# Log-sum-exp over rows: the first load read as one block, its results stored early, and the semaphores cleared under the last store

## The chip, the cores and the metric

The kernel runs on one core of a Trainium2 chip. The metric is the device time of one execution in microseconds (us); less is better. The span that the profile shows runs from the first to the last instruction of the program; the time is about 1.8 us longer.

Engines are named as in the profile: ACT is ScalarE, DVE is VectorE, POOL is GpSimd, SP is SyncE; a name with a q (SPq) is that engine's queue of DMA issues, waits and semaphore instructions.

## The reference

```python
x = np.random.randn(32, 512, 1024).astype(np.float32)      # 67.1 MB
def reference(x, axis):                                    # axis = -1
    x_max = np.max(x, axis=axis, keepdims=True)
    return (x_max.squeeze(axis) + np.log(np.sum(np.exp(x - x_max), axis=axis))).astype(np.float32)
```

There are 16,384 rows of 4 KiB, and one number comes out of each. The kernel leaves the maximum out and computes log(sum(exp(x))) directly.

## The kernel before

Partition p owns rows 128p to 128p+127 (`p t` below), so the same row number of two neighbouring partitions lies 512 KiB apart in HBM. The rows come in 17 chunks of 16 down to 1 rows per partition, all loaded by SP into a ring of 51 rows. For each chunk ACT takes the exponential; the first `n_dve` rows are summed by DVE, the others by ACT itself (`accum_out`). Two logarithms turn the sums into results: the first covers chunks 0 to 4 and is taken when chunk 5 starts, the second covers the rest. One store writes everything.

```python
CHUNKS = [(4, 1), (15, 11), (16, 10), (16, 15), (16, 0), (14, 0), (12, 9), (9, 5), (7, 5), (5, 4),
          (4, 3), (3, 0), (2, 2), (2, 2), (1, 0), (1, 0), (1, 0)]       # (rows, of them for DVE)
x_v = x_flat.rearrange("(p t) d -> p t d", p=P)
out_v = bass.AP(tensor=out.tensor, offset=out.offset, ap=[[NB, P], [1, NB]])      # NB = 128
landed = [tc.alloc_semaphore(f"landed{i}") for i in range(len(CHUNKS))]           # and three more
# ... (cut: load(i) waits on SP until the ring's rows are free, then issues chunk i)
nc.sync.dma_start(out=ring[:, s : s + r], in_=x_v[:, row : row + r]).then_inc(landed[i], 16)
# ... (cut: exponentials, sums, logarithms)
nc.scalar.dma_start(out=out_v, in_=res).then_inc(stored, 16)
nc.gpsimd.wait_ge(stored, 16)
# the tile context closes: barrier, clear its semaphores, barrier
```

The softmax here doesn't subtract the row's maximum and nothing guards it: scores larger than these inputs give would overflow.

Of the kernel before, what the change touches and what calls it, by code (L numbers as in the profile page):

```python
# [1 line left out]

# [4 lines left out]



CHUNKS = [  # L10
    (4, 1), (15, 11), (16, 10), (16, 15), (16, 0), (14, 0), (12, 9), (9, 5), (7, 5), (5, 4),
    (4, 3), (3, 0), (2, 2), (2, 2), (1, 0), (1, 0), (1, 0),
]
RING_ROWS = 51

LN_AT = 5

FIRST_PARTS = [("sync", 0, 128)]


@with_exitstack
def kernel(
    ctx: ExitStack,
    tc: tile.TileContext,
    x: bass.AP,
    axis: bass.AP,
    out: bass.AP,
):
    nc = tc.nc
    P = nc.NUM_PARTITIONS  # L30

    assert axis in (-1, len(x.shape) - 1), f"only last-axis reduction supported, got {axis}"

    x_flat = x.flatten_outer_dims()
    N, D = x_flat.shape
    assert N % P == 0
    NB = N // P
    assert sum(r for r, _ in CHUNKS) == NB

    fp32 = mybir.dt.float32  # L40
    Exp = mybir.ActivationFunctionType.Exp
    Ln = mybir.ActivationFunctionType.Ln
    AX = mybir.AxisListType.X

    x_v = x_flat.rearrange("(p t) d -> p t d", p=P)
    out_v = bass.AP(tensor=out.tensor, offset=out.offset, ap=[[NB, P], [1, NB]])

    ring = nc.alloc_sbuf_tensor("ring", [P, RING_ROWS, D], fp32).ap()
    sums = nc.alloc_sbuf_tensor("sums", [P, NB], fp32).ap()
    res = nc.alloc_sbuf_tensor("res", [P, NB], fp32).ap()  # L50

    landed = [tc.alloc_semaphore(f"landed{i}") for i in range(len(CHUNKS))]
    act_done = tc.alloc_semaphore("act_done")
    dve_done = tc.alloc_semaphore("dve_done")
    stored = tc.alloc_semaphore("stored")


    hook = nc.pop_inst_callback()
    symbolic, nc._always_lower_symbolic_ap = nc._always_lower_symbolic_ap, False


    place = []
    row = slot = 0
    for r, _ in CHUNKS:
        if slot + r > RING_ROWS:
            slot = 0
        place.append((slot, row))
        slot += r
        row += r



    busy = [(0, 0)] * RING_ROWS
    acts = dves = 0

    def load(i):
        (s, row), r = place[i], CHUNKS[i][0]
        act_wait = max(a for a, _ in busy[s : s + r])
        dve_wait = max(d for _, d in busy[s : s + r])
        if dve_wait:  # L80
            nc.sync.wait_ge(dve_done, dve_wait)
        if act_wait:
            nc.sync.wait_ge(act_done, act_wait)
        for engine, lo, hi in FIRST_PARTS if i == 0 else [("sync", 0, P)]:
            getattr(nc, engine).dma_start(
                out=ring[lo:hi, s : s + r], in_=x_v[lo:hi, row : row + r]
            ).then_inc(landed[i], 16)

    def take_logs(lo, hi, dve_wait, act_wait):
        nonlocal acts  # L90
        nc.scalar.wait_ge(act_done, act_wait)
        nc.scalar.wait_ge(dve_done, dve_wait)
        nc.scalar.activation(out=res[:, lo:hi], in_=sums[:, lo:hi], func=Ln).then_inc(  # L93
            act_done, 1
        )
        acts += 1

    body = nc.main_func.blocks[-1]
    assert not body.instructions
    load(0)  # L100
    n_early = len(body.instructions)

    nc.scalar.preload_act_table_set("natural_log_exp_and_others")  # L103

    logged = 0
    done_before = [(0, 0)]
    for i, (r, n_dve) in enumerate(CHUNKS):
        if i:
            load(i)
        s, row = place[i]  # L110
        if i == LN_AT:
            logged = row
            take_logs(0, logged, *done_before[i])
        nc.scalar.wait_ge(landed[i], 16 * (len(FIRST_PARTS) if i == 0 else 1))
        if n_dve:
            nc.scalar.activation(  # L116
                out=ring[:, s : s + n_dve], in_=ring[:, s : s + n_dve], func=Exp
            ).then_inc(act_done, 1)
            acts += 1
            nc.vector.wait_ge(act_done, acts)  # L120
            nc.vector.reduce_sum(  # L121
                out=sums[:, row : row + n_dve], in_=ring[:, s : s + n_dve], axis=AX
            ).then_inc(dve_done, 1)
            dves += 1
            for j in range(n_dve):
                busy[s + j] = (0, dves)
        for j in range(n_dve, r):
            nc.scalar.activation(  # L128
                out=ring[:, s + j],
                in_=ring[:, s + j],  # L130
                func=Exp,
                accum_out=sums[:, row + j : row + j + 1],
            ).then_inc(act_done, 1)
            acts += 1
            busy[s + j] = (acts, 0)
        done_before.append((dves, acts))

    take_logs(logged, NB, dves, acts)
    nc.scalar.wait_ge(act_done, acts)
    nc.scalar.dma_start(out=out_v, in_=res).then_inc(stored, 16)  # L140
    nc.gpsimd.wait_ge(stored, 16)



    first = nc.main_func.blocks[0]
    head, work = first.instructions, body.instructions
    end = next(k for k, i in enumerate(head) if i.opcode == "UnconditionalBranch")
    head, tail = head[:end], head[end:]
    for ins in work[:n_early]:
        at = next(  # L150
            k for k, i in enumerate(head) if i.engine == ins.engine and i.opcode == "Drain"
        )
        head.insert(at, ins)
    first.instructions = head + work[n_early:] + tail
    body.instructions = []

    nc._always_lower_symbolic_ap = symbolic
    nc.push_inst_callback(hook)


# [1 line left out]
_INS = ['x', 'axis']  # L162
_OUTS = [((32, 512), 'float32')]

_NUMBERS = {'axis': -1}


# [26 lines left out]
```

## Time and profile before

| | before |
|---|---|
| time, median of the first 3 runs | 164.23 us (164.02 to 164.56) |
| span of the profiled run | 162.18 us |
| chunk 0 landed | 7.40 us |
| chunk 4 landed; ACT without idle time from here on | 83.67 us |
| chunk 16, the last, landed | 158.08 us |
| last store issued; GpSimd past its wait | 159.64; 161.24 us |
| end of the closing barriers | 162.18 us |

The landing times are those of the last of each load's 16 semaphore steps in the trace. First come lines of the profile's page, for the whole run: the busy engines, then the DMA queues with packets, MB and their share of 16 engines' span.

```profile
span 162.2 us, 213 instructions
...
DVE 72.9 (45%) x11; ACT 124.1 (76%) x136; POOL 0.2 (0%) x4
...
q1 hardware_dynamic: 2448, 67.11, 96.4%
q10 hardware_dynamic: 144, 0.07, 0.1%
q14 instruction: 1, 0.01, 0.0%
```

The load queue q1 is busy for 96.4% of the span, and ACT for 76%. The next view is the chain of waits in order of time (start us, us, what).

```profile
47.15 36.52 DMA ring<-in_x_dram
83.67 0.02 issue
83.69 10.55 ACT ring L128 x21
...
156.21 2.71 ACT ring L128 x5
158.91 0.22 issue
159.14 0.20 ACT ring L128
```

The chain goes through loads until chunk 4 lands, then through ACT. That looks like an ACT-bound second half. But the loads run level with it: the last chunk lands at 158.08 us and ACT takes it at 158.19. Now the stage table around the events that the change touches (stretch, its length, busy time with counts of DVE, ACT and POOL, clock, DMA share, GB/s). The table counts a packet's bytes where the packet starts, so a short stretch is to be compared with the same stretch of another run and not with a rate.

```profile
0.70:2.70 2.00, 0.00 (x0) 1.28 (x1) 0.00 (x0) 1.00 0.77 262
...
147.00:149.00 2.00, 2.00 (x1) 2.00 (x2) 0.00 (x0) 1.00 0.95 399
```

Last, the close, as instructions of the line that ends the kernel (duration in ns min/median/max, first and last start in us).

```profile
L189 POOLq EVENT_SEMAPHORE  x4: 17/17/17, 161.5 to 162.1; - x4
...
L189 POOLq COMPARE_BRANCH  x1: 33/33/33, 161.2 to 161.2; - x1
L189 POOLq EVENT_SEMAPHORE_RANGE_CLEAR  x1: 139/139/139, 161.7 to 161.7; - x1
```

Four semaphore instructions of GpSimd are two barriers, a gather and a release each, with the range clear between them. From GpSimd's passing at 161.24 us to the end it takes 0.94 us.

### The profile page before, as it was taken

What the parts mean: (1) busy time and instruction counts of PE and PEld (TensorE: products, weight loads), DVE (VectorE), ACT (ScalarE), POOL (GpSimd) and SP (SyncE); (2) the same over time, 40 slices, a digit from 0 to 9 for tenths busy, and PEclk for the clock granted to TensorE, in tenths of its full rate; (3) what the DMA queues carried; (4) which work ended last, traced back from release to release, by engine and by line L of the source; (5) the groups of instructions that cost most, each with busy time, mean ns of one, the idle gap of its engine ahead of it and who ended that gap; (6) DMA issues with size and microseconds to landing.
All of it is one profiled execution on the core that took longest, in us unless ns stands there. A gap on an engine that the chain in (4) does not pass through costs nothing.

```text
span 162.2 us, 213 instructions
## 1 busy us (share of the span) xinstructions
DVE 72.9 (45%) x11; ACT 124.1 (76%) x136; POOL 0.2 (0%) x4
## 2 busy tenths in 40 slices
DVE  0030000039960799000999900000006999799591
ACT  3180006997099971999339999999999999999993
POOL 0000000000000000000000000000000000000000
DMA  6999899969969959969988999999999999999970
GB/s 263 497 485 470 349 394 517 485 291 517 485 291 517 517 259 517 517 275 501 517 368 370 424 424 432 461 497 388 436 427 399 431 400 439 420 424 414 415 318 16
DMA packets 2593, 67.18 MB, mean 414 GB/s; under 512 B 288, under 2 KB 416, under 8 KB 800
## 3 DMA queue, kind: packets, MB, share of 16 engines
q1 hardware_dynamic: 2448, 67.11, 96.4%
q10 hardware_dynamic: 144, 0.07, 0.1%
q14 instruction: 1, 0.01, 0.0%
HBM read 67.11 MB, written 0.07 MB: 414 GB/s over the span
## 4 chain that ended last, share of the span: by engine, by line
ACT 52%; DMA 38%; DVE 7%; issue 1%
DMA ring<-in_x_dram 38%; ACT ring L128 30%; ACT ring L116 22%; DVE sums L121 7%; ACT res L93 0%
## 5 line engine op out<-in xcount | busy, mean ns | idle before, releaser
L121 DVE TENSOR_REDUCE sums<-ring 128x5 f32<-128x5120 f32 (+8 forms) x11 | 72.9, 6648 | 86.0 <-ACT ring L116 85.9
L116 ACT ACTIVATE ring<-ring 128x5120 f32<-128x5120 f32 (+8 forms) x11 | 59.3, 5394 | 29.4 <-DMA ring<-in_x_dram 29.4
L128 ACT ACTIVATE ring<-ring 128x1024 f32<-128x1024 f32 x61 | 63.4, 1041 | 5.3 <-DMA ring<-in_x_dram 5.3
L128 ACT ACTIVATION_READ_ACCUMULATOR ring<-ring 128x1 f32 x61 | 11.4, 187 | 0.0
L103 ACT ACT_TABLE_LOAD x1 | 1.3, 1283 | 0.8 <-PEq L175 0.8
L93 ACT ACTIVATE res<-sums 128x67 f32<-128x67 f32 (+1 forms) x2 | 0.5, 256 | 0.1
L175 POOL MEMSET const-bfloat16-1.0<- 128x1 bf16 x1 | 0.1, 101 | 0.0
L175 POOL MEMSET const-uint8-127<- 128x1 uint8 x1 | 0.1, 101 | 0.0
L175 POOL MEMSET const-float32-0.0<- 128x1 f32 x1 | 0.1, 98 | 0.2 <-issue 0.2
L175 POOL MEMSET const-float32-1.0<- 128x1 f32 x1 | 0.1, 98 | 0.0
## 6 DMA issues: line engine op xcount, KB each, us to landing
ring<-in_x_dram SPq DMA_DIRECT2D x1, 7680.0 KB, 24.8
ring<-in_x_dram SPq DMA_DIRECT2D x1, 7168.0 KB, 36.1
ring<-in_x_dram SPq DMA_DIRECT2D x1, 6144.0 KB, 21.6
ring<-in_x_dram SPq DMA_DIRECT2D x1, 4608.0 KB, 32.1
ring<-in_x_dram SPq DMA_DIRECT2D x2, 2048.0 KB, 26.3
ring<-in_x_dram SPq DMA_DIRECT2D x1, 3584.0 KB, 40.2
ring<-in_x_dram SPq DMA_DIRECT2D x1, 2560.0 KB, 44.4
ring<-in_x_dram SPq DMA_DIRECT2D x2, 1024.0 KB, 46.0
```

What stands on the lines that cost most here:

```text
L93: nc.scalar.activation(out=res[:, lo:hi], in_=sums[:, lo:hi], func=Ln).then_inc(act_done, 1)
L103: nc.scalar.preload_act_table_set("natural_log_exp_and_others")
L116: nc.scalar.activation(out=ring[:, s : s + n_dve], in_=ring[:, s : s + n_dve], func=Exp).then_inc(act_done, 1)
L121: nc.vector.reduce_sum(out=sums[:, row : row + n_dve], in_=ring[:, s : s + n_dve], axis=AX).then_inc(dve_done, 1)
L128: nc.scalar.activation(out=ring[:, s + j], in_=ring[:, s + j], func=Exp, accum_out=sums[:, row + j : row + j + 1],).then_inc(act_done, 1)
L175: nc = _bacc.Bacc("TRN2", target_bir_lowering=False, num_devices=1)
```

## The change

The intent: make the first load contiguous so that it starts faster; get the results of its rows out early; and clear the semaphores while the last store is on its way, so that less is left to do after it. Chunk 0 is now rows 0 to 511 of the input (rows 4p to 4p+3 for partition p, one block of 2 MB); the other rows follow at 508 KiB pitch. So the results fall into two pieces of the output, stored as 16-byte and as 496-byte rows, packed one after another.

```diff
-    x_v = x_flat.rearrange("(p t) d -> p t d", p=P)
-    out_v = bass.AP(tensor=out.tensor, offset=out.offset, ap=[[NB, P], [1, NB]])
+    R0 = CHUNKS[0][0]                                                    # 4
+    x_first = x_flat[: P * R0].rearrange("(p t) d -> p t d", p=P)
+    x_rest = x_flat[P * R0 :].rearrange("(p t) d -> p t d", p=P)
+    out_first = bass.AP(tensor=out.tensor, offset=out.offset, ap=[[R0, P], [1, R0]])
+    out_rest = bass.AP(
+        tensor=out.tensor, offset=out.offset + P * R0, ap=[[NB - R0, P], [1, NB - R0]]
+    )
...
-    landed = [tc.alloc_semaphore(f"landed{i}") for i in range(len(CHUNKS))]
+    landed = [nc.alloc_semaphore(f"landed{i}") for i in range(len(CHUNKS))]   # the others likewise
...
+        if i == STORE_AT:                                                # 11, ahead of load(11)
+            nc.sync.wait_ge(act_done, logs_done)
+            nc.sync.dma_start(out=out_first, in_=res[:, :R0]).then_inc(stored_first, 16)
         if i:
             load(i)
...
-    nc.scalar.dma_start(out=out_v, in_=res).then_inc(stored, 16)
-    nc.gpsimd.wait_ge(stored, 16)
+    nc.scalar.dma_start(out=out_rest, in_=res[:, R0:]).then_inc(stored, 16)
+    nc.scalar.sem_clear(range(used[0], used[-1] + 1))
+    for sem in (stored_first, stored):
+        nc.gpsimd.wait_ge(sem, 16)
+        nc.gpsimd.sem_inc(sem, -16)
```

More of the change, by code (lines that the diff above doesn't have):

```diff
@@ L16 @@
 LN_AT = 5
-FIRST_PARTS = [("sync", 0, 128)]
+STORE_AT = 11
 @with_exitstack
@@ L43, with rows_of @@
     AX = mybir.AxisListType.X
-    x_v = x_flat.rearrange("(p t) d -> p t d", p=P)
-    out_v = bass.AP(tensor=out.tensor, offset=out.offset, ap=[[NB, P], [1, NB]])
+    R0 = CHUNKS[0][0]
[5 more added lines that the diff above has]
+    )
+    def rows_of(row, r):
+        return x_first if row == 0 else x_rest[:, row - R0 : row - R0 + r]
     ring = nc.alloc_sbuf_tensor("ring", [P, RING_ROWS, D], fp32).ap()
@@ L50 @@
     res = nc.alloc_sbuf_tensor("res", [P, NB], fp32).ap()
-    landed = [tc.alloc_semaphore(f"landed{i}") for i in range(len(CHUNKS))]
-    act_done = tc.alloc_semaphore("act_done")
-    dve_done = tc.alloc_semaphore("dve_done")
-    stored = tc.alloc_semaphore("stored")
+    landed = [nc.alloc_semaphore(f"landed{i}") for i in range(len(CHUNKS))]
+    act_done = nc.alloc_semaphore("act_done")
+    dve_done = nc.alloc_semaphore("dve_done")
+    stored_first = nc.alloc_semaphore("stored_first")
+    stored = nc.alloc_semaphore("stored")
+    used = sorted(sem.num for sem in [*landed, act_done, dve_done])
+    assert used == list(range(used[0], used[0] + len(used)))
     hook = nc.pop_inst_callback()
@@ L83, in load @@
             nc.sync.wait_ge(act_done, act_wait)
-        for engine, lo, hi in FIRST_PARTS if i == 0 else [("sync", 0, P)]:
-            getattr(nc, engine).dma_start(
-                out=ring[lo:hi, s : s + r], in_=x_v[lo:hi, row : row + r]
-            ).then_inc(landed[i], 16)
+        nc.sync.dma_start(out=ring[:, s : s + r], in_=rows_of(row, r)).then_inc(landed[i], 16)
     def take_logs(lo, hi, dve_wait, act_wait):
@@ L113 @@
             take_logs(0, logged, *done_before[i])
-        nc.scalar.wait_ge(landed[i], 16 * (len(FIRST_PARTS) if i == 0 else 1))
+            logs_done = acts
+        nc.scalar.wait_ge(landed[i], 16)
         if n_dve:
```

## The prediction

> **What bounds it now.** The span is 162.18 us; the run takes about 2 us more, outside it. From start to end the kernel is paced by one stream of loads: 67.11 MB of 67.18 moved, and the stage table gives 416, 436, 439, 426, 425 GB/s in the stages up to 116 us. From the trace's landings, the three 16-row chunks land 19.36, 19.39 and 19.33 us apart (8.39 MB each, 433 GB/s); a 61,440-byte packet takes 2.267 us, the same rate times 16. The chain of waits hands over to ScalarE at 83.69 us, when chunk 4 lands, and ScalarE is then busy until 159.61 (idle: 0.0x us). The two are level: in the timeline chunk 10 lands 0.13 us before ScalarE takes it, chunk 11 0.14, chunk 13 about 0.03, chunk 16 0.11. So a delay of the whole load stream passes to the end nearly one for one, and so does an advance. Before 7.42 us ScalarE waits for chunk 0, after 159.64 nothing but the store and the closing ceremony is left.
>
> **Terms.**
> 1. Chunk 0 as one block. Packets of 16,384 bytes take 0.611 us in the steady state, but the first two on each engine took up to 1.36 us; the excess sums to 5.9 us, 0.37 us per engine. Now rows lie 512 KiB apart. The Trainium skill, "DMA: Bandwidth & Descriptors", section "Latency and other measured facts", says that power-of-two row pitches slow copies (slightly at 512 KiB, much at megabytes), with aliasing of channels as an inference. This trace agrees only in the start: the steady rate is at full speed, so the 508 KiB pitch of the rest should gain nothing. I take 0.25 us of the 0.37 off; chunk 0 then lands at about 7.1 instead of 7.40, and chunk 4 and everything after moves with it. Critical.
> 2. The early store: 128 descriptors of 16 bytes in the load queue before chunk 11, 8 per engine. A 4-byte packet takes 9 ns, a 512-byte one 27 ns: estimate 0.07 to 0.25 us per engine, say 0.15, in a stream without slack. Critical, a cost.
> 3. The last store has rows of 496 bytes instead of 512. The same page, "Specifications", has a read-modify-write under 512 bytes; no run here shows it yet. Before: issue 159.64, landed 161.22. Estimate +0.1 us. Critical.
> 4. The close. After the landing GpSimd passes at 161.24, a first barrier ends at about 161.66, then a drain, a range clear (139 ns), a drain and a second barrier end at 162.18. With no semaphores of the context left to clear I expect clear and second barrier to go: -0.5 us (if the second barrier stays, only -0.17). GpSimd gains two decrements after its waits: +0.06. The clear on ScalarE (139 ns) after the issue at 160.01 hides under the 1.2 us until landing.
>
> Sum: -0.25 + 0.15 + 0.1 - 0.5 + 0.06 = -0.44 us.
>
> **Prediction:** 163.8 us, range 163.2 to 164.4. Faster by over 2%: 0.02; within 2%: 0.97; slower by over 2%: 0.01.
>
> **What would show it.** (1) First packets near 0.61 us, chunk 0 landing at 7.0 to 7.2, chunk 4 earlier by the same. (2) Chunk 10 to 11 landing gap 3.69 now, 3.8 to 3.9 after; small ScalarE idle times near chunks 11 to 16. (3) issue-to-landing of the last store 1.57 us now, 1.6 to 1.8 after. (4) one barrier after the landing, 0.45 us instead of 0.94 from GpSimd's passing to the end.
>
> **What would make it wrong.** The slow start is the cost of a cold engine and not of the pitch; tiny HBM writes stall the load ring by much more than their packets; partial rows in the last store take far longer; the second barrier stays; or the runs' own scatter (164.02 to 164.56) swallows 0.4 us.

## The result

The changed kernel took 164.51 us (median of 6 runs, 164.39 to 164.76), the kernel before in the same rounds and the earlier runs 164.43 us (6 runs, 164.02 to 164.56). The ratio is 1.0011 with a 95% interval of 0.9997 to 1.0024: no change at 2%, and if anything 0.1% slower. A ratio is always the mean time of one kernel's fast runs over that of the other's of the same rounds, so it is not quite the ratio of the medians. The predicted 163.8 us, with a range to 164.4, was too fast: the 0.44 us gain did not come.

The page after, the same lines:

```profile
span 162.8 us, 214 instructions
...
DVE 72.9 (45%) x11; ACT 124.2 (76%) x136; POOL 0.2 (0%) x4
...
q1 hardware_dynamic: 2592, 67.11, 96.6%
q10 hardware_dynamic: 144, 0.06, 0.1%
```

The engines do the same work. q1 has 144 more packets: the early store, 128 of data and 16 of semaphore. The chain of waits after:

```profile
64.87 36.40 DMA ring<-in_x_dram
101.28 0.02 issue
101.30 3.23 ACT ring L142 x6
104.53 0.02 issue
104.55 45.56 DMA ring<-in_x_dram
150.11 0.02 issue
150.13 3.23 ACT ring L142 x6
```

The chain now waits for loads at two places more, chunk 5 at 101.28 us and chunk 11 at 150.11 us. So the loads fell behind ACT. The stage table after:

```profile
0.70:2.70 2.00, 0.00 (x0) 1.28 (x1) 0.00 (x0) 1.00 0.93 197
...
147.00:149.00 2.00, 2.00 (x1) 2.00 (x2) 0.00 (x0) 1.00 1.01 346
```

Less moved in the first 2 us (197 against 262 GB/s), although the DMA engines are busy for more of it: the packets are stretched. Less is moved between 147 and 149 us too, in chunk 11, which follows the early store in the queue (346 against 399). The close:

```profile
L157 ACTq EVENT_SEMAPHORE_RANGE_CLEAR  x1: 119/119/119, 160.8 to 160.8; - x1
L160 POOLq EVENT_SEMAPHORE  x2: 17/17/17, 146.9 to 162.2; - x2
L208 POOLq EVENT_SEMAPHORE  x4: 17/17/17, 162.3 to 162.7; - x4
```

The clear has moved to ACT, at 160.8 us under the store. But GpSimd still has four semaphore instructions at the end: both barriers are still there. From GpSimd's passing at 162.17 us to the end it takes 0.68 us instead of 0.94.

Where the 0.66 us between these two profiles went, from landings and starts in the trace:

| event | before | after | later by |
|---|---|---|---|
| chunk 0 landed | 7.40 | 7.73 | 0.33 |
| chunk 4 landed | 83.67 | 83.94 | 0.26 |
| chunk 5 landed | 100.65 | 101.28 | 0.63 |
| chunk 10 landed | 145.61 | 146.23 | 0.62 |
| chunk 11 landed | 149.30 | 150.11 | 0.82 |
| chunk 16 landed | 158.08 | 158.85 | 0.77 |
| last store, issue to GpSimd's passing | 1.60 | 1.74 | 0.15 |
| from there to the end | 0.94 | 0.68 | -0.26 |

So there are three losses on the loads (start, between chunk 4 and 5, between chunk 10 and 11), one at the last store, and one gain. The pair of profiles overstates the difference: the runs' means differ by 0.18 us, while the profiled run before took 163.96 us, its fastest. The experiments therefore take more profiles of each layout and time each part.

One more reading is needed, by packet. The trace lists every DMA packet with start and duration. On each of the 16 engines one load packet follows another without a gap, so each engine's sequence can be followed through the run. The one exception is the instruction fetch: while its packet runs, 0.30 us long, its engine carries no load packet. In both kernels the load packet just after it, of chunk 5, is stretched as well:

```
kernel   instruction packet     load packet of chunk 5 (57,344 bytes, usual 2116 to 2120 ns)
before   89.05 us, 8,192 bytes  89.35 us, 2379 ns; its engine was the 3rd of 16 to finish chunk 4, 0.62 us ahead of the last
after    89.54 us, 8,192 bytes  89.85 us, 2498 ns; its engine was the 10th, 0.22 us ahead of the last
```

So the fetch costs its engine about 0.57 us before and 0.68 us after: 0.30 for itself, the rest for the stretched packet. The chunk lands later only by what exceeds that engine's lead over the last one: nothing before (0.57 against 0.62), 0.46 us after (0.68 against 0.22).

### The profile page after: what moved, and what is told of

It is laid out like the page before. It is cut to its first block, busy times and chain, and to the rows that moved or that the text cites. A ratio compares the mean times of both kernels' runs of the same rounds, so it can differ in the third digit from the quotient of the medians.

```text
span 162.8 us, 214 instructions
## 1 busy us (share of the span) xinstructions
DVE 72.9 (45%) x11; ACT 124.2 (76%) x136; POOL 0.2 (0%) x4
## 4 chain that ended last, share of the span: by engine, by line
DMA 77%; ACT 14%; DVE 7%; issue 0%; SPq 0%
DMA ring<-in_x_dram 77%; ACT ring L130 8%; DVE sums L135 7%; ACT ring L142 6%; SPq L97 0%; ACT res L103 0%
```

## The experiments

Two theories stood at the start. **A**: the losses belong to the change, each to one of its parts (block, tiny packed rows in the load queue, packed rows in the last store), and the fetch hurts because the block leaves its engine among the late ones. **B**: the losses are scatter of single runs, and the parts cost nothing. Each kernel got one profile; those with rounds were timed against the kernel before on the same chip. "Excess" is the duration of chunk 0's packets over 611 ns each, summed and divided by 16 engines.

| run | excess of chunk 0 | chunk 0 / chunk 4 landed | gap of landings, chunk 10 to 11, first step / last step | last store | close | ratio to before (95%) |
|---|---|---|---|---|---|---|
| before | 0.36 | 7.40 / 83.67 | 3.69 / 3.69 | 1.60 | 0.94 | |
| before_again | 0.47 | 7.42 / 83.75 | 3.69 / 3.71 | 1.60 | 0.94 | one look |
| close_only | 0.55 | 7.41 / 83.74 | 3.70 / 3.70 | 1.61 | 0.68 | 0.9982 (0.9969 to 0.9994) |
| old_rows | 0.58 | 7.30 / 83.88 | 3.71 / 3.71 | 1.60 | 0.68 | 0.9990 (0.9978 to 1.0002) |
| packed_stores | 0.56 | 7.57 / 83.88 | 3.75 / 3.95 | 1.64 | 0.68 | 1.0015 (0.9994 to 1.0036) |
| block_read_only | 0.83 | 7.61 / 83.79 | 3.69 / 3.69 | 1.60 | 0.94 | 1.0006 (0.9992 to 1.0020) |
| block_close | 0.82 | 7.69 / 83.86 | 3.69 / 3.68 | 1.61 | 0.68 | 0.9986 (0.9973 to 0.9999) |
| store_last | 0.91 | 7.58 / 83.77 | 3.68 / 3.69 | 1.74 | 0.68 | 0.9993 (0.9980 to 1.0006) |
| after | 0.94 | 7.73 / 83.94 | 3.89 / 3.88 | 1.74 | 0.68 | 1.0011 (0.9997 to 1.0024) |
| after_again | 0.84 | 7.68 / 83.87 | 3.93 / 3.71 | 1.74 | 0.68 | one look |

(Excess, landings, gaps, store and close in us, each from one profile.) The kernels that give wrong results are marked below. The comparison with the reference passed them all the same, because the rows' results lie too close together to tell rows apart; nothing here rests on their results.

### A second look at both kernels

No edit.

> A second profile of the kernel before, to see what is the kernel's and what is the run's. Theory A (the slow start and the lag belong to the layout): chunk 0 lands at 7.3 to 7.5 us, excess of the 16,384-byte packets of chunk 0 over 611 ns about 0.36 us per engine as in the first profile, and the instruction fetch of 8,192 bytes near 89 us costs nothing at chunk 5's landing (spread of its 16 semaphore steps about 0.7 us). Theory B (both are scatter of the run): chunk 0 lands anywhere from 7.2 to 7.9 us, and the spread of chunk 5 can be 1 us here too.

> A second profile of the changed kernel. Theory A: chunk 0 lands again at 7.6 to 7.8 us, excess 0.8 to 1.0 us per engine, chunk 5's landing again spread over about 1 us. Theory B: somewhere between 7.2 and 7.9 us with no relation to the kernel. Either way the landing gap of chunks 10 to 11 stays near 3.88 us (3.69 before) and the close takes 0.67 us from GpSimd's passing to the end.

Measured: theory A for the start. Chunk 0 landed at 7.42 us in the kernel before and at 7.68 us in the changed one; the excess was 0.47 and 0.84 us. For the lag at chunk 5 too: the fetch's engine was again the 3rd to finish chunk 4 before, 0.77 us ahead of the last, and the 10th after, 0.32 us ahead; it made chunk 5 late by 0.36 us after (its end against that of the latest other engine) and by nothing before. The last-to-last gap of chunks 10 to 11 was 3.71 us after, not 3.88 as expected, while the first-to-first gap was 3.93: the stall hits most engines, and how much of it reaches the last one varies. In this look the last engine was the one delayed by the fetch.

### The block alone

The kernel before with chunk 0 read from the first 2 MB (wrong: `x_0` holds rows of other partitions):

```diff
+    x_0 = x_flat[: P * 4].rearrange("(p t) d -> p t d", p=P)
-                out=ring[lo:hi, s : s + r], in_=x_v[lo:hi, row : row + r]
+                out=ring[lo:hi, s : s + r],
+                in_=x_0[lo:hi, 0:r] if i == 0 else x_v[lo:hi, row : row + r],
```

> The kernel before with one edit: chunk 0 is read from the first 2 MB as one block (wrong result on purpose, the rows are those of other partitions); stores, close and the other loads as before. Theory A: chunk 0 lands 0.25 to 0.35 us later than in the kernel before, and the time rises by 0.3 to 0.6 us (0.6 if the lag on one engine at chunk 5 comes with it). Theory B: same time within 0.15 us. The prediction's own theory (the block starts faster): time falls by 0.25 us.

Measured: 164.41 us (5 runs) against 164.28 (9 runs), ratio 1.0006 (0.9992 to 1.0020). The start is slow again (excess 0.83 us, chunk 0 at 7.61), and the fetch again meets an engine with a small lead (0.34 us) and costs 0.33 us in the profile. The 0.25 us gain that the prediction took for the block would be a ratio of 0.9985, which is outside the interval. But theory A's 0.3 to 0.6 us did not come either; the cost in time is small and not clear of zero.

### The close alone

```diff
-    stored = tc.alloc_semaphore("stored")       # the others likewise
+    stored = nc.alloc_semaphore("stored")
+    nc.scalar.sem_clear(range(used[0], used[-1] + 1))      # used: numbers of all of them but `stored`
     nc.gpsimd.wait_ge(stored, 16)
+    nc.gpsimd.sem_inc(stored, -16)
```

> The kernel before with only the new way of clearing semaphores. From the profile after: GpSimd's passing to the end 0.67 instead of 0.94 us, so the time falls by 0.25 us (0.15%); the store's issue to landing stays at 1.57 us. If the gain of the close is eaten by the decrement behind the wait or by the clear on ScalarE: no change.

Measured: 164.00 us against 164.28, ratio 0.9982 (0.9969 to 0.9994), clear of no change. The close took 0.68 instead of 0.94 us and the store 1.61 us. The lines of its close:

```profile
L193 POOLq EVENT_SEMAPHORE  x4: 17/17/17, 161.6 to 162.0; - x4
...
L143 ACTq EVENT_SEMAPHORE_RANGE_CLEAR  x1: 119/119/119, 160.2 to 160.2; - x1
```

This part of the change works. It saves the clear, a drain around it and GpSimd's branch, and keeps the second barrier.

### The early store behind the loads

The changed kernel, with the first store issued after the last load. Its wait is left out, since the last load's wait covers it; a wait left at the end would race with the clear.

```diff
-        if i == STORE_AT:
-            nc.sync.wait_ge(act_done, logs_done)
-            nc.sync.dma_start(out=out_first, in_=res[:, :R0]).then_inc(stored_first, 16)
...
+    nc.sync.dma_start(out=out_first, in_=res[:, :R0]).then_inc(stored_first, 16)
     take_logs(logged, NB, dves, acts)
```

> The changed kernel with the early store of 128 times 16 bytes moved behind all loads in the same queue (its wait is covered by that of the last load, so it is left out). If the early store stalls the loads: landing gap of chunk 10 to 11 back from 3.88 to 3.69 us, all later chunks 0.15 to 0.2 us earlier, time down by 0.1 to 0.2 us against the changed kernel (164.5 to 164.35). If the stall only fills slack of engines that are ahead (in the second profile of the changed kernel the last landing did not move against chunk 10): the gap changes and the time does not. No 12,288-byte packet over 0.6 us in either case.

Measured: gaps of 3.68 and 3.69 us, no 12,288-byte packet of chunk 11 over 0.5 us (20 of them in the first profile after), and 164.17 us (5 runs) against 164.31 (11 runs) before, ratio 0.9993. Against the changed kernel's 1.0011, from another session, that is 0.18% or 0.3 us less, more than expected; the two intervals overlap a little. The stage from 147 to 149 us, the counterpart of the lines above:

```profile
147.00:149.00 2.00, 2.00 (x1) 2.00 (x2) 0.00 (x0) 1.00 1.01 426
```

### The old row map with both stores

The changed kernel with 512 KiB pitch for all chunks. The early store stays at the same place, but its 16-byte rows now lie 512 bytes apart, and the last store's 496-byte rows too.

```diff
+    x_v = x_flat.rearrange("(p t) d -> p t d", p=P)
# ... (cut: all loads read x_v)
-    out_first = bass.AP(tensor=out.tensor, offset=out.offset, ap=[[R0, P], [1, R0]])
-    out_rest = bass.AP(..., offset=out.offset + P * R0, ap=[[NB - R0, P], [1, NB - R0]])
+    out_first = bass.AP(tensor=out.tensor, offset=out.offset, ap=[[NB, P], [1, R0]])
+    out_rest = bass.AP(tensor=out.tensor, offset=out.offset + R0, ap=[[NB, P], [1, NB - R0]])
```

> The changed kernel with the old row map: chunk 0 and the rest both at 512 KiB pitch, so the block is undone and the early store, the last store of 496 bytes and the new close stay. If the block costs: chunk 0 lands at 7.4 instead of 7.7 us, excess 0.36 to 0.55 us per engine instead of 0.8 to 0.95, the spread of chunk 5's landing 0.7 to 0.9 us instead of 1.0 to 1.1, time down by 0.2 to 0.4 us against the changed kernel, that is 0.0 to 0.2 us under the kernel before. If the block costs nothing in time (its run alone was within 0.2%): same as the changed kernel. The last store: 1.72 us from issue to landing if 496 bytes do it, 1.57 if it was rows that share a 512-byte line.

Measured: 164.12 us (6 runs) against 164.31, ratio 0.9990. Chunk 0 landed at 7.30 us with an excess of 0.58 us, as expected. Two surprises. First, the same 128 descriptors of 16 bytes at the same place of the queue caused no stall at all: gaps of 3.71 us, no stretched packet, and 399 GB/s as in the kernel before:

```profile
147.00:149.00 2.00, 2.00 (x1) 2.00 (x2) 0.00 (x0) 1.00 0.94 399
```

Also the last store of 496 bytes took 1.60 us, as 512 bytes do. So it is not the size of the rows. Second, the spread of chunk 5's landing was 1.25 us here, not 0.7 to 0.9: the fetch met an engine only 0.27 us ahead of the last and cost 0.38 us. A small lead of that engine is not the block's alone.

### Packed stores without the block

The kernel of the last run, with the store addresses of the changed kernel (wrong: rows land in wrong places).

```diff
-    out_first = bass.AP(tensor=out.tensor, offset=out.offset, ap=[[NB, P], [1, R0]])
-    out_rest = bass.AP(tensor=out.tensor, offset=out.offset + R0, ap=[[NB, P], [1, NB - R0]])
+    out_first = bass.AP(tensor=out.tensor, offset=out.offset, ap=[[R0, P], [1, R0]])
+    out_rest = bass.AP(..., offset=out.offset + P * R0, ap=[[NB - R0, P], [1, NB - R0]])
```

> The run old_rows with one edit: both stores write packed rows (16 bytes every 16, 496 every 496) as in the changed kernel, loads at 512 KiB pitch (wrong result on purpose, rows land in the wrong places). If the packing is what costs (old_rows, with rows 512 bytes apart, showed no stretched packets and a last store of 1.60 us): some ten 12,288-byte packets of 0.6 to 1.3 us again, first-to-first landing gap of chunk 10 to 11 3.89 us instead of 3.71, last store 1.72 to 1.75 us from issue to GpSimd's passing; time up by 0.15 to 0.3 us against old_rows. If it is the block's load layout that makes the stall: gap 3.71 and no stretched packets here.

Measured: 164.56 us (6 runs, 164.21 to 165.27) against 164.41 (11 runs), ratio 1.0015 (0.9994 to 1.0036). The stall is back, with 22 stretched packets of chunk 11 (0.52 to 0.97 us instead of 0.46) and a last-to-last gap of 3.95 us. The expected first-to-first gap of 3.89 was only 3.75. In time it is 0.25% or 0.4 us over the run before it, more than expected, but the two were timed against the kernel before on different chips and their intervals just overlap. The stage line:

```profile
147.00:149.00 2.00, 2.00 (x1) 2.00 (x2) 0.00 (x0) 1.00 0.95 328
```

So the packed rows make the stall, whatever the loads' layout. The stall comes late: the last 16-byte packet ends at 145.47 us and the store's last semaphore step is at 146.52, while 20 of the 22 stretched packets start between 147.4 and 148.7 us. The profiles of the changed kernel show the same order. What holds these packets up so long after is not shown. For the last store the expectation missed: 1.64 us, not 1.72 to 1.75. Packing raised it, but by 0.04 us here and by 0.12 to 0.15 us in the four profiles with the block (1.72 to 1.74); what makes the rest is open. The packets are not slower: in every profile the store's packets take 27 ns on average and 0.35 to 0.36 us from first to last. What grows is the time from the end of the last data packet to the last semaphore step: 0.35 us with rows 512 bytes apart, 0.39 us here, 0.47 to 0.50 us with packed rows and the block.

### The block with the new close

The kernel of "the close alone" with chunk 0 read as a block, so without any change of the stores (wrong; the edit is that of "the block alone").

> The run close_only with chunk 0 read as one 2 MB block (wrong result on purpose): the changed kernel without any change of the stores. If the block costs what the block alone showed in time (+0.06%, in doubt): 0.1 us over close_only, so 0.15 to 0.2 us under the kernel before (ratio 0.9985 to 0.999). If the later landing of chunk 0 (0.25 to 0.3 us) passes to the end whole: no gain left over the kernel before (ratio 1.000). Chunk 0 lands at 7.55 to 7.75, chunk 4 at 83.75 to 83.95 us.

Measured: 164.18 us (6 runs, 164.13 to 164.25) against 164.41, ratio 0.9986 (0.9973 to 0.9999). Taken with 0.9982 of the close alone, the block costs 0.04% or 0.07 us; taken alone, 0.06% or 0.1 us. Neither is clear of zero. Chunk 0 landed at 7.69 and chunk 4 at 83.86 us: of the 0.27 us behind the close alone at the start, 0.12 us is left at chunk 4.

### The fetch moved

The changed kernel with 24 small logarithms on ACT, put where it waits for chunk 1 anyway:

```diff
+        if i == 1:
+            pad = nc.alloc_sbuf_tensor("pad", [P, 24], fp32).ap()
+            nc.scalar.wait_ge(act_done, acts)
+            for j in range(24):
+                nc.scalar.activation(out=pad[:, j : j + 1], in_=sums[:, 1:2], func=Ln)
```

> The changed kernel with 24 small activations on ScalarE after chunk 0, while it waits for chunk 1 anyway. Theory (an instruction fetch of ScalarE delays one DMA engine, which is a late one after the block start): the 8,192-byte instruction packet moves from 89.5 us to an earlier time (before chunk 4, at 25 to 83 us), the one load packet stretched by 0.38 us moves with it, and the spread of landing steps grows to about 1 us from that chunk on instead of from chunk 5 on. Rival (something of chunk 5's load, such as its issue or the start of a short chunk): fetch moves or not, the stretched packet stays in chunk 5 near 89.7 us.

Measured: the 8,192-byte instruction packet came at 49.16 us instead of 89.5. The one load packet stretched between chunk 0 and chunk 11 was now at 49.46 us (2749 instead of 2418 ns); no packet of chunk 5 was stretched by more than 40 ns. The spread of chunk 3's landing grew to 0.93 us, from 0.58 and 0.77 in the two profiles of the changed kernel. Theory A holds: ACT's instruction fetch delays one DMA engine, here by 0.66 us (0.30 for the fetch, 0.33 for the stretched packet, the rest scatter), and the delay stays on that engine. It need not be a late one: here it was the 2nd to finish chunk 2, 0.46 us ahead of the last, and chunk 3 came 0.19 us late.

### Other pitches of the first load

As in "the block alone", with `x_0 = x_flat[: P * k]` and k = 127, 8 and 32 rows (wrong on purpose), one look each.

> The kernel before with chunk 0 read at a pitch of 127 rows (508 KiB) instead of 128 (wrong result on purpose). If the slow start at 512 KiB comes from the power of two (the prediction's theory): excess of chunk 0's packets falls from 0.36 to 0.55 us per engine to below 0.2. If a cold start costs it whatever the pitch: still 0.35 to 0.55. In the block it was 0.83 to 0.94.

> The kernel before with chunk 0 read at 32 KiB pitch (wrong result on purpose). If near addresses are what slows the start: excess of chunk 0 between the block's 0.83 to 1.03 us per engine and the 0.36 to 0.66 of 508 and 512 KiB. If only the seamless block does it: 0.4 to 0.6. Whatever the excess, if a fast start is paid for later, chunk 4 lands at 83.65 to 83.95 us.

> The kernel before with chunk 0 read at 128 KiB pitch (wrong result on purpose). Near addresses: excess below that of 32 KiB and above 0.36. Seamless block only: 0.4 to 0.6. Chunk 4 as in the other pitches.

| pitch of chunk 0 | excess of chunk 0, us per engine | chunk 0 landed | chunk 4 landed | time of the one run |
|---|---|---|---|---|
| 16 KiB, the block (six profiles) | 0.82 to 1.03 | 7.58 to 7.73 | 83.77 to 83.94 (84.11 where the fetch came earlier) | |
| 32 KiB | 0.66 | 7.30 | 83.66 | 164.14 |
| 128 KiB | 0.59 | 7.23 | 83.48 | 164.17 |
| 508 KiB | 0.66 | 7.28 | 83.87 | 164.35 |
| 512 KiB (five profiles) | 0.36 to 0.58 | 7.30 to 7.57 | 83.67 to 83.88 | |

The prediction's reason for the slow start, the power of two, falls: 508 KiB starts no faster than 512 (its excess of 0.66 us lies above both expected ranges). Only the seamless block stands out; twice its pitch is already like 508 KiB, in one look each. A ramp of about half a microsecond is there at every pitch. That 128 KiB might be the best start is a hint from one look.

The trace also shows why the block's late start is not paid in full. In chunks 1 to 4 the other layouts have further packets stretched by more than 60 ns, 6 to 22 of them per profile at 512 KiB. The block's profiles have 0 or 1, apart from the one that the fetch makes. What the first load does not pay at once is partly paid later. Why this is so was not tested.

## Why the prediction was wrong

**What bounds it: right.** The load stream sets the end. In all fourteen profiles the last logarithm starts 1.28 to 1.31 us after the last chunk lands, whether that is at 158.08 or at 158.85 us.

**Term 1, the block: wrong in sign, the main error.** The step that failed is "I take 0.25 us of the 0.37 off". The excess rose from 0.36 to 0.94 us, and chunk 0 landed 0.33 us later instead of 0.3 earlier; over all profiles the excess is 0.82 to 1.03 us with the block and 0.36 to 0.58 us at 512 KiB. Why a seamless block starts slower was not tested. The step's ground was the Trainium skill's note on row pitches in powers of two ("DMA: Bandwidth & Descriptors", section "Latency and other measured facts"); it gives 207 GB/s for copies at 512 KiB pitch and 214 as full. The trace before had already shown the steady loads at full rate at that pitch, so only the ramp was left to explain, and the run at 508 KiB shows that the power of two does not explain it. In time the block costs about 0.1 us, not clear of zero, where -0.25 was taken: an error of about 0.3 us.

**Term 2, the early store: its size fair in the gap, its reason wrong.** Predicted 0.15 us from the packets' own durations. The 16-byte packets take 9 ns each; what costs is the loads behind them, stretched from 0.46 to as much as 1.34 us, most of them 1.8 to 3.2 us after the last 16-byte packet ended. The last-to-last gap grew by 0.0 to 0.26 us over the four profiles with packed rows ahead of chunk 11 (after, after_again, act_pads, packed_stores). Rows 512 bytes apart cost nothing that the one profile shows. That writes to neighbouring bytes get in each other's way is a guess; no run shows the mechanism, nor why the stall comes so late.

**Term 3, the last store: right in size.** Predicted +0.1 us, measured +0.04 to 0.15 us. The reason given was rows below 512 bytes (the same page, section "Specifications"), and that is not what this shows: 496-byte rows at 512 bytes' distance took 1.60 us, as before. Packed rows cost it, between the last packet and the last semaphore step.

**Term 4, the close: mis-sized.** Predicted -0.44 us net, on "I expect clear and second barrier to go". The second barrier stayed. Measured: -0.26 us in the profile, -0.28 us in the medians of the close alone. The prediction named this as a risk, but its figure for that case (-0.17 + 0.06 = -0.11 us) was too small.

**Not foreseen: the instruction fetch.** It was in the profile before, as one line of q14, and was passed over because it cost nothing there. The Trainium skill, "Runtime: NRT & Kernel Launch", section "Instruction fetch mechanics", calls the cost of crossing a block boundary mostly hidden. Here it costs its DMA engine 0.53 to 0.68 us in every profile, and is hidden only when that engine has a larger lead over the last one. In the five unpadded profiles with the block the lead was 0.22 to 0.34 us, and chunk 5 came 0.33 to 0.46 us late; in the five at 512 KiB it was 0.62 to 0.77 us four times, with a cost of 0 to 0.02 us, and 0.27 us once, with 0.38 us. The other pitches lie between (lead 0.25 to 0.47 us, cost 0.15 to 0.42 us), so the small lead is not the block's alone, and what sets it was not tested. The timed runs do not show a block cost of that size. A likely reason is that ordinary runs of the kernel before meet it too: they scatter from 163.96 to 164.83 us, and its two profiled runs, in which the fetch cost nothing, took 163.96 and 164.01 us, at the low end. But the other runs have no profile, so this is argued only.

The sum with measured terms: block +0.1, early store about +0.15 (from the gaps; the times of its runs would give 0.3 to 0.4 us, across sessions), last store +0.1, close -0.28, together about +0.1 us. Measured by the means: +0.18 us, with an interval of -0.05 to 0.39 us.

The best version is the kernel before with the new close alone: 164.00 us against 164.28, ratio 0.9982, the lowest of all runs here, with an interval clear of one; the profile's close shows the same 0.26 us. It was not timed beside the changed kernel; each was timed beside the kernel before.

## What to carry to other kernels

When a stream of loads sets the end, what is put into that queue can be paid at the end, and its price is what happens to the packets behind it, not its own packets: keep small stores out of it, or at least keep their rows apart. A bulk load lands with its slowest DMA engine, so compare a delay of one engine with that engine's lead before taking it for hidden or for harmless. Split a change into its parts before keeping it: here one part gained 0.28 us and the others gave it back.

## What the Trainium skill lacked or had wrong

- "DMA: Bandwidth & Descriptors", "Specifications": it warns of transfers below 512 bytes. Here 496-byte rows at 512 bytes' distance stored as fast as 512-byte rows (1.60 and 1.60 us), and 16-byte rows 512 bytes apart did not disturb the loads (gap 3.71 against 3.69 us). The same rows packed did: 20 and 22 load packets of 460 ns stretched to as much as 1338 ns.
- The same page, "Latency and other measured facts": for a pitch of 512 KiB it gives 207 GB/s per direction in copies. Loads alone ran at 433 GB/s at that pitch (8.39 MB in 19.36 us), which does not contradict a figure per direction of a copy; and 508 KiB did not start faster. The page does not say that the first packets of a load ramp up (0.36 to 1.03 us of excess per engine), nor that one seamless block ramps slowest.
- The same page, "Where 436 GB/s comes from": it says that the HBM side, about 358 GB/s, binds for transfers from HBM to SBUF. One core's loads ran at 433 GB/s here, close to the 435 of its other limit, so the sentence does not hold for a core that streams alone; the same page's measured table, for one core with the other of its pair idle, has 425 GB/s and fits.
- "Runtime: NRT & Kernel Launch", "Instruction fetch mechanics": it calls the fetch's cost mostly hidden and its blocks 16 KiB. Here a fetch of 8,192 bytes took 309 ns on one load engine and stretched the next load packet there by 0.25 to 0.38 us, 0.53 to 0.68 us together; where that engine had a smaller lead over the last one, the chunk landed up to 0.46 us late.
